# A plain second matmul in superblock 0, and zero matmuls at the start, in a one-core MLP kernel

## Chip, cores and metric

The kernel runs on one core of one Trainium2 chip. The metric is the device time of one execution in microseconds, the median of several runs.

## What is computed

Inputs are float32: x of 8 x 1024 x 1024, w1 of 1024 x 4096 and w2 of 4096 x 1024.

```python
h = x @ w1
h = 0.5 * h * (1 + np.tanh(np.sqrt(2 / np.pi) * (h + 0.044715 * h ** 3)))
return (h @ w2).astype(np.float32)
```

## The kernel before

**Superblocks and products.** The 8192 rows of x are worked off in 8 superblocks (sb) of 1024 rows. Each has two matrix products: `matmul1` gives g = gelu(x w1), kept in SBUF as four float16 blocks g11, g12, g21, g22, and `matmul2` gives the output rows. Both split their operands in 2 x 2 blocks and use a seven-product recursion: seven block products of sums and differences take the place of eight. `A_TERMS` lists the differences of the left operand, `B_TERMS` the sums of the weights; products 2 and 5 use plain weight blocks (`PLAIN`), the other five need sums (`SUMS`). One block product of a superblock is 64 matmuls of 128 x 128 by 128 x 512, so a stage is 448 matmuls. In `matmul2` from superblock 2 on, products 6 and 7 (`INNER`) are themselves split once more by `inner_product`, whose weight sums `split_inner` writes to DRAM (`in_d`) in superblock 1.

**matmul1.** It runs over 16 column chunks c of w1, four to a quad. Each chunk uses three of the eight PSUM banks (pb, qb, rb) and does 28 matmuls. ScalarE copies pb out to a tmp tile, VectorE combines tmp tiles and banks, ScalarE applies GELU. A chunk's last product (6) is done inside the next chunk (`finish`). tmp tiles come from a pool of ten, which the stores of the output also use. In superblock 0 w1 arrives as float32 in staging tiles from the pool `gc` (four buffers), is cast to float16 by ScalarE and POOL, is summed by VectorE, and its raw blocks are written to `raw_d`. Superblock 1 reads `raw_d`, makes the sums again and writes them to `w1_d` on POOL's queue. Later superblocks read `w1_d` and the plain blocks of `raw_d` (`load_ops`).

**matmul2.** Superblocks 0 and 1 use `matmul2_made`. In superblock 0 `bring` loads w2 in float32 in the order in which the products 4, 2, 5, 1, 7, 3, 6 need it, POOL casts it, `add` makes each product's sums on VectorE just ahead, and `keep` writes the raw blocks to `raw2_d`. Superblock 1 reads `raw2_d`, makes the sums a second time, writes them to `w2_d`, and splits the operands of products 7 and 6. Superblocks 2 to 7 use `matmul2` with `load_ops` from `w2_d` and `raw2_d`.

**What sets the order.** Each engine takes its instructions in a fixed order that a scheduler lays down at build time; `keep_in_program_order` (in `load_in_order`) holds SP's DMAs to the program's order, and `issue_after` puts an instruction behind another one. SP's queue carries the loads, x's transposes from DRAM (`x_transpose`) and the raw writes; POOL's queue carries the output stores, the writes of `w1_d`, `w2_d` and `in_d`, and the cast of x to float16 (`x_cast`). All share the same 16 DMA engines. An operand tile (`unit`) is one of 26 buffers of 128 x 2048 float16, 0.52 MB. At the end of superblock 0 the order on SP is: the last loads of w2, 16 transposes of x for superblock 1, eight writes of `raw2_d`, then the reads of `raw_d` for superblock 1.

**The start.** `x_first` loads superblock 0's rows in eight pieces q (four with a = 1, then four with a = 0) and transposes them on TensorE against an identity; ScalarE and VectorE copy the banks out. The first matmul follows when the first columns of w1 are cast and summed (`load_cols`).

Of the kernel before, what the change touches and what calls it, by code (L numbers as in the profile page):

```python
# [56 lines left out]
def kernel(  # L57
# [42 lines left out]
    raw2_d = [dram.tile([P, 4, QC * OH], DT, name=f"raw2_d{q}") for q in range(NI // QC)]  # L100
# [38 lines left out]
    def cast_in(dst, src, cast, staged=False):  # L139
        if staged:  # L140
            st = up.tile([P] + list(dst.shape[1:]), F32, name="u")
        else:
            st = gcp.tile([P] + list(dst.shape[1:]), F32, name="gc")
        load_in_order(st, src)
        cast(out=dst, in_=st)
# [52 lines left out]
    def load_ops(d, raw, ms, rows, cols):  # L198

        ops = {}  # L200
        for m in ms:
            t = unit(rows, cols)
            src = raw[:, BLOCKS.index(B_TERMS[m][0]), :] if m in PLAIN else d[:, m - 1, :]
            nc.sync.dma_start(out=flat(t), in_=src)
            ops[m] = t
        return ops
# [18 lines left out]

    def x_first():
        identity = consts.tile([P, P], F32, name="identity")
        make_identity(nc, identity)
        blocks = x_blocks()
        xs = XOps(blocks)  # L230
        for a in (1, 0):
            for q in range(NQ):
# [3 lines left out]
                for k in (1, 0):  # L236
                    ps = psum()
                    for j in range(KH):
                        nc.tensor.matmul(
                            ps[:, j * P:(j + 1) * P],  # L240
                            lhsT=xn[:, k, j * P:(j + 1) * P],
                            rhs=identity,
                            is_transpose=True,
                            start=(j == 0),
                            stop=(j == KH - 1),
                        )
                    eng = nc.vector.tensor_copy if k == 0 else nc.scalar.copy
                    eng(
                        out=blocks[f"{a + 1}{k + 1}"][:, :, q * P:(q + 1) * P],
                        in_=ps.rearrange("p (j t) -> p j t", t=P),  # L250
                    )
            if a:
                xs.make(2)
# [23 lines left out]
    def matmul1(xs, sb):  # L277
# [14 lines left out]
        def gelu(b, c, src):  # L292
            nc.scalar.activation(out=g[b][:, c, :], in_=src, func=GELU)  # L293
# [11 lines left out]
        def ahead(q, step):  # L305
# [3 lines left out]
            if sb > 1:  # L309
                if step == 0:  # L310
                    quads.append(load_ops(w1_d[q], raw_d[q], ORDER, KH, QW))
                return
# [6 lines left out]
            for m in ((), (4,), (1, 3), (7, 6))[step]:  # L319
                quads[q].sum(m)  # L320

# [59 lines left out]
    def matmul2_made(sb, g, keep_w1):  # L381


        raw = {b: [] for b in BLOCKS}
        sums = {}
        blocks = None

        def bring(bs, staged):
            for q in range(NI // QC):
                for b in bs:  # L390
                    t = unit(QC, OH)
                    raw[b].append(t)
                    if sb:
                        nc.sync.dma_start(out=flat(t), in_=raw2_d[q][:, BLOCKS.index(b), :])
                        continue
                    for j in range(0, QC, 2):
                        c = q * QC + j
                        cast_in(
                            t[:, j:j + 2, :],
                            w2v[int(b[1]) - 1, int(b[0]) - 1, :, c:c + 2, :],  # L400
                            pool_copy,
                            staged,
                        )
                if q == 0 and keep_w1 is not None and "11" in bs:
                    keep_w1()

        def keep(bs):
            if sb == 0:
                for b in bs:
                    for q in range(NI // QC):  # L410
                        load_in_order(raw2_d[q][:, BLOCKS.index(b), :], flat(raw[b][q]))

        def add(m):
            u, op, v = B_TERMS[m]
            sums[m] = []
            for q in range(NI // QC):
                t = unit(QC, OH)
                tt(t, raw[u][q], raw[v][q], op)
                sums[m].append(t)
                if sb:  # L420
                    nc.gpsimd.dma_start(out=w2_d[q][:, m - 1, :], in_=flat(t))

        def pieces(m):
            return raw[B_TERMS[m][0]] if m in PLAIN else sums[m]

        def copy_out(b, q, ps):
            c = temp()
            nc.scalar.copy(out=c, in_=ps)
            return store(sb, b, q, c), c

        v, c21 = {}, {}
        pb, qb, rb = [], [], []
        bring(("11", "21"), False)
        add(4)
        for q, ps in product2(g, 4, pieces(4), pb, True, True):
            v[q] = temp()
            nc.scalar.copy(out=v[q], in_=ps)
        bring(("22",), True)
        if sb == 0:
            xb = x_cast(1, pool_last[0])  # L440
        keep(("11", "21"))
        for q, ps in product2(g, 2, pieces(2), pb, False):
            _, c21[q] = copy_out("21", q, ps)
        add(1)
        u, d = halves()[1], halves()[1]
        for q, ps in product2(g, 5, pieces(5), qb, True):
            tt(u[q], v[q], ps, SUB)
            tt(d[q], u[q], c21[q], SUB)
        add(7)
        bring(("12",), True)  # L450
        for q, ps in product2(g, 1, pieces(1), rb, True):
            tt(d[q], d[q], ps, ADD)
        if sb == 0:
            blocks = x_transpose(xb, load_in_order)
        keep(("22", "12"))
        for q, ps in product2(g, 7, pieces(7), rb, False):
            c = temp()
            tt(c, u[q], ps, ADD)
            store(sb, "11", q, c)
        if sb:  # L460
            split_inner(7, pieces(7))
        add(3)
        add(6)
        for q, ps in product2(g, 3, pieces(3), qb, False):
            copy_out("12", q, ps)
        for q, ps in product2(g, 6, pieces(6), qb, False):
            c = temp()
            tt(c, d[q], ps, ADD)
            last = store(sb, "22", q, c)
        if sb:  # L470
            split_inner(6, pieces(6))
# [89 lines left out]
    def product2(g, m, pieces, banks, first, by_chunk=False):  # L561

        u, v = A_TERMS[m]

        def mm(q, a, c):
            nc.tensor.matmul(  # L566
                banks[q],
                lhsT=a,
                rhs=pieces[c // QC][:, c % QC, :],
                start=(first and c == 0),  # L570
                stop=(c == NI - 1),
                skip_group_check=not first,
            )

        if first:
            banks.extend(psum() for _ in range(NQ))
        if by_chunk:
            for c0 in range(0, NI, QC):
                for q in range(NQ):
                    for c in range(c0, c0 + QC):  # L580
                        mm(q, g[u][:, c, q * P:(q + 1) * P], c)
                    if c0 + QC == NI:
                        yield q, banks[q]
            return
        for q in range(NQ):
            cols = slice(q * P, (q + 1) * P)
            a = g[u][:, :, cols]
            if v is not None:
                a = gcp.tile([P, NI, P], GT, name="gc")
                tt(a, g[u][:, :, cols], g[v][:, :, cols], SUB)  # L590
            for c in range(NI):
                mm(q, a[:, c, :], c)
            yield q, banks[q]

    def halves():
        tiles = [up.tile([P, 2, OH], F32, name="u") for _ in range(2)]
        return tiles, [tiles[q // 2][:, q % 2, :] for q in range(NQ)]

    def matmul2(sb, g):
        def product(m, banks, first):  # L600
            pieces = [load_ops(w2_d[q], raw2_d[q], (m,), QC, OH)[m] for q in range(NI // QC)]
            return product2(g, m, pieces, banks, first)
# [7 lines left out]
        x6 = inner_x(6, g)  # L610
# [8 lines left out]
        inner_product(6, x6, d2)  # L619
        x7 = inner_x(7, g)  # L620
        for q, ps in product(3, qb, False):
            c12 = temp()
            nc.scalar.copy(out=c12, in_=ps)  # L623
            store(sb, "12", q, c12)
            tt(d[q], d[q], ps, ADD)
        for q, ps in product(1, rb, True):
            tt(u[q], u[q], ps, ADD)
            tt(d[q], d[q], ps, ADD)
            store(sb, "22", q, d[q])
        inner_product(7, x7, u2)  # L630
        for q in range(NQ):
            last = store(sb, "11", q, u[q])
        return last

    warm = consts.tile([P, 1], F32, name="warm")
# [3 lines left out]
    for sb in range(NSB):  # L639
        g, quad = matmul1(xs, sb)  # L640
        if sb and sb + 1 < NSB:
            blocks = x_transpose(x_cast(sb + 1, last), nc.sync.dma_start)
        if sb == 0:
            last, blocks = matmul2_made(sb, g, quad.keep_raw)
        elif sb == 1:
            last, _ = matmul2_made(sb, g, None)
        else:
            last = matmul2(sb, g)
# [33 lines left out]
```

## Time and profile before

| | |
|---|---|
| median of 3 runs | 1586.64 us (1584.47 to 1587.4) |
| the profiled execution's own time | 1586.64 us |
| its span, first to last instruction | 1584.9 us |
| TensorE busy | 1551.0 us, 98% |
| VectorE, ScalarE, POOL busy | 64%, 29%, 14% |
| mean granted TensorE clock | 0.994 |
| DMA | 358.93 MB, mean 226 GB/s |

PE is TensorE, PEld its weight loads, DVE VectorE, ACT ScalarE, SPq the queue of SyncE. A line of a timeline has the start, the length, the engine, the line of the code, the operation, output <- input, the count, and in brackets the idle time before it and what ended that. Stages, by the start of their first matmul: superblock 0's matmul1 at 17.52 us, its matmul2 at 122.67, superblock 1's at 220.78 and 328.18, superblock 2's at 425.59 and 529.80.

### The profile page before, as it was taken

To read this page: it belongs to the slowest core of one execution; us is meant where nothing else is said; L and a number is where in the kernel's file an instruction comes from. 1 tells how busy PE (TensorE), PEld (TensorE's weight loads), DVE (VectorE), ACT (ScalarE), POOL (GpSimd) and SP (SyncE) were. 2 spreads that over 40 slices of the span, in tenths; PEclk is the share of its full clock that TensorE was granted. 3 is DMA by queue.
4 is the path that set the end of the run, shared out by engine and by line. 5 is a ranking of instruction groups with operands and counts; after the bars stand their busy time and mean duration, and the time that the engine had idled before them with its cause. 6 is when DMAs were issued, how large, how long until landed. Compare 5 with 4: busy or idle time off the path is not lost.

```text
span 1584.9 us, 20386 instructions
## 1 busy us (share of the span) xinstructions
PE 1551.0 (98%) x7808; PEld 768.0 (48%) x7808; DVE 1010.9 (64%) x1263; ACT 457.7 (29%) x776; POOL 222.6 (14%) x306
## 2 busy tenths in 40 slices
PE   7999989999989999999999999999999999999998
PEld 4444434444434455444554445544555445544455
DVE  6877767667755566555675557656475556755564
ACT  4641014520144211441124410344103430044200
POOL 2244222012400013000120001200012001200000
PEclk9999999999999999999999999999999999999999
DMA  9998698645984467735686346954469545663155
GB/s 304 337 325 281 180 371 281 203 179 197 385 300 133 186 239 259 255 97 200 252 281 224 121 171 252 336 176 180 152 243 362 153 166 191 242 257 133 54 212 186
DMA packets 167362, 358.93 MB, mean 226 GB/s; under 512 B 72928, under 2 KB 79072, under 8 KB 166368
## 3 DMA queue, kind: packets, MB, share of 16 engines
q1 hardware_dynamic: 148672, 285.26, 51.3%
q0 software_dynamic: 18592, 72.37, 13.9%
q8 instruction: 61, 1.00, 0.2%
q14 instruction: 37, 0.30, 0.1%
HBM read 278.92 MB, written 93.32 MB: 235 GB/s over the span
## 4 chain that ended last, share of the span: by engine, by line
PE 85%; DMA 8%; DVE 4%; issue 2%; ACT 1%; POOL 0%; SPq 0%; DVEq 0%; ACTq 0%; POOLq 0%
PE ps L283 44%; PE ps L566 35%; PE ps L522 6%; DVE u L112 2%; DMA out_dram<-tmp 2%; DMA u<-w_d 2%; DMA gc<-in_w_dram 1%; DMA u<-raw_d 1%; DMA in_d<-u 1%; DVE tmp L112 1%; DMA u<-in_d 1%; DVE gc L112 0%; ACT g L293 0%; DMA u<-in_x_dram 0%; POOL in_d L487 0%
## 5 line engine op out<-in xcount | busy, mean ns | idle before, releaser
L283 PE MATMUL ps<-u 128*128 128x512 f16 x3584 | 784.2, 381 | 20.5 <-DVE tmp L112 15.3
L112 DVE TENSOR_TENSOR tmp<-tmp,ps 128x512 f32<-128x512 f32 x548 | 375.5, 687 | 307.4 <-ACT tmp L347 119.9
L283 PEld LDWEIGHTS <-u 128*128 128x128 f16 x3584 | 351.7, 98 | 450.8 <-issue 29.5
L566 PE MATMUL ps<-u,gc 128*128 128x512 f16 x1792 | 389.4, 379 | 0.0
L566 PEld LDWEIGHTS <-gc 128*128 128x128 f16 x1792 | 175.3, 98 | 211.5
L293 ACT ACTIVATE g<-tmp 128x512 f16<-128x512 f32 x256 | 161.0, 630 | 296.7 <-DVE tmp L112 296.7
L566 PE MATMUL ps<-u,g 128*128 128x512 f16 x1024 | 224.4, 379 | 0.4 <-DVE u L112 0.2
L293 ACT ACTIVATE g<-ps 128x512 f16<-128x512 f32 x256 | 151.9, 596 | 102.3 <-PE ps L283 102.1
L112 DVE TENSOR_TENSOR u<-u 128x2048 f16<-128x2048 f16 (+2 forms) x150 | 162.9, 1122 | 20.5 <-DMA u<-raw_d 12.5
L566 PEld LDWEIGHTS <-g 128*128 128x128 f16 x1024 | 100.2, 98 | 120.7 <-issue 1.9
L112 DVE TENSOR_TENSOR gc<-g,g 128x2048 f16<-128x2048 f16 x112 | 136.7, 1253 | 20.5 <-PE ps L566 20.5
L379 POOL DMA_DIRECT2D out_dram<-tmp x72 | 39.6, 551 | 778.3 <-ACT tmp L616 632.3
L112 DVE TENSOR_TENSOR u<-u,ps 128x512 f32<-128x512 f32 x152 | 101.2, 682 | 71.1 <-ACT tmp L623 37.3
L522 PE MATMUL ps<-u,gc 128*128 128x256 f16 x960 | 110.6, 274 | 0.8
L522 PEld LDWEIGHTS <-gc 128*128 128x128 f16 x960 | 94.4, 98 | 13.3 <-issue 1.9
L347 ACT COPY tmp<-ps 128x512 f32<-128x512 f32 x128 | 73.0, 570 | 93.6 <-PE ps L283 93.6
L112 DVE TENSOR_TENSOR gc<-u 128x2048 f16<-128x2048 f16 x60 | 73.2, 1221 | 38.9 <-PE ps L566 38.9
L112 DVE TENSOR_TENSOR tmp<-ps,tmp 128x512 f32<-128x512 f32 x128 | 88.4, 690 | 9.7 <-DMA out_dram<-tmp 4.0
L112 DVE TENSOR_TENSOR u<-tmp,ps 128x512 f32<-128x512 f32 x32 | 22.0, 687 | 83.6 <-PE ps L566 73.9
L112 DVE TENSOR_TENSOR u<-g,g 128x2048 f16<-128x2048 f16 x48 | 59.6, 1280 | 0.0
L616 ACT COPY tmp<-ps 128x512 f32<-128x512 f32 x24 | 14.1, 587 | 151.9 <-PE ps L566 151.9
L545 POOL TENSOR_TENSOR u<-u,tmp 128x512 f32<-128x512 f32 x12 | 26.2, 2180 | 200.1 <-DMA u<-in_d 141.4
(33 smaller groups left out, 354.1 us busy)
## 6 DMA issues: line engine op xcount, KB each, us to landing
u<-w_d SPq DMA_DIRECT2D x192, 512.0 KB, 8.3
u<-raw_d SPq DMA_DIRECT2D x128, 512.0 KB, 8.1
u<-in_d SPq DMA_DIRECT2D x84, 512.0 KB, 7.2
gc<-in_w_dram SPq DMA_DIRECT2D x48, 512.0 KB, 6.2
w_d<-u POOLq DMA_DIRECT2D x40, 512.0 KB, 6.9
out_dram<-tmp POOLq DMA_DIRECT2D x72, 256.0 KB, 3.1
raw_d<-u SPq DMA_DIRECT2D x32, 512.0 KB, 7.5
xb<-in_x_dram POOLq DMA_DIRECT2D x56, 256.0 KB, 11.4
```

Of the source, the lines that this page charges most:

```text
L112: nc.vector.tensor_tensor(out=out, in0=in0, in1=in1, op=op)
L283: nc.tensor.matmul(bank, lhsT=ops[m][:, k, cs], rhs=xs[m][:, k, :], start=(first and k == 0), stop=(k == KH - 1), skip_group_check=not first,)
L293: nc.scalar.activation(out=g[b][:, c, :], in_=src, func=GELU)
L347: nc.scalar.copy(out=v, in_=pb)
L379: return queue.dma_start(out=out2[r0:r0 + P, o0:o0 + OH], in_=src)
L522: nc.tensor.matmul(bank[:, i * HO:(i + 1) * HO], lhsT=t[:, c, i * P:(i + 1) * P], rhs=y[j][:, c, :], start=(first and i == 0 and c == 0), ...
L545: nc.gpsimd.tensor_tensor(out=part("11"), in0=part("11"), in1=pair(u), op=ADD)
L566: nc.tensor.matmul(banks[q], lhsT=a, rhs=pieces[c // QC][:, c % QC, :], start=(first and c == 0), stop=(c == NI - 1), skip_group_check=not ...
L616: nc.scalar.copy(out=c21, in_=ps)
```

## The change

- Superblock 0's second matmul (`matmul2_first` in place of `matmul2_made`) is a plain product: two halves b of the output columns, each with eight PSUM banks (all there are), 16 chunks c of w2 rows and both row halves a: 512 matmuls. The last three chunks (`TAIL`) are done bank by bank, and ScalarE copies each bank out as it ends. w2 arrives half by half in the `gc` staging buffers. POOL casts the first two quads of half 0; ScalarE casts all else, and only after the last GELU (`act_late_copy`).
- In half 1 VectorE makes all five sums of each quad, and SP writes all seven operands to `w2_d`: quads 0 and 1 between the loads, quads 2 and 3 behind x's transposes. `raw2_d` is gone.
- Superblock 1's second matmul is now `matmul2`, which reads `w2_d`. It does its products in the order 4, 5, 2, 3, 1, 6, 7 without the inner recursion, and splits the operands of 6 and 7 for later superblocks. x for superblock 2 is transposed as for the later ones.
- `matmul1` of superblock 1 also writes the two plain operands of each quad to `w1_d` (`copy_plain`, 8 writes more); later superblocks read all seven from there.
- `keep_clock` issues matmuls on a zero tile into one PSUM bank: 8 before the first transposes, 2 after each piece of x, 6 after the last piece.

```diff
+    def act_late_copy(out, in_):
+        with tc.issue_after(gelu_last[0].ins):
+            nc.scalar.copy(out=out, in_=in_)
...
+        def copy_plain(self):
+            for m in PLAIN:
+                nc.gpsimd.dma_start(out=w1_d[self.q][:, m - 1, :], in_=flat(self.ops[m]))
...
+    def keep_clock(bank, n):
+        for _ in range(n):
+            tc.keep_in_program_order(
+                nc.tensor.matmul(bank, lhsT=idle[:, :P], rhs=idle, start=True, stop=True)
+            )
...
+        idle_bank = psum()
+        keep_clock(idle_bank, 8)
...
+                keep_clock(idle_bank, 2 if a or q < NQ - 1 else 6)
...
+            if sb == 1 and step == 3:
+                quads[q].copy_plain()
...
+    def matmul2_first(sb, g, keep_w1):
+        TAIL = 3
...
+        def write(q):
+            for m in SUMS + PLAIN:
+                load_in_order(w2_d[q][:, m - 1, :], flat(made[q][m]))
+
+        for b in range(2):
+            banks = [psum() for _ in range(2 * NQ)]
+            ready = []
...
+            for q in range(NI // QC):
+                raw = raw_units(QC, OH, (b + 1,))
+                for j in range(0, QC, 2):
+                    c = q * QC + j
+                    for a in range(2):
+                        cast_in(
+                            raw[f"{a + 1}{b + 1}"][:, j:j + 2, :],
+                            w2v[b, a, :, c:c + 2, :],
+                            pool_copy if b == 0 and q < 2 else act_late_copy,
+                        )
+                for j in range(QC):
+                    w = [raw[f"{a + 1}{b + 1}"][:, j, :] for a in range(2)]
+                    ready.append(w)
+                    if q * QC + j < NI - TAIL:
+                        for i in range(2 * NQ):
+                            mm(i, q * QC + j, w)
+                if b == 0:
+                    keep.append(raw)
+                    if q == 0:
+                        keep_w1()
+                    elif q == 1:
+                        xb = x_cast(1, pool_last[0])
+                else:
+                    ops = {}
+                    for m in SUMS + PLAIN:
+                        make_sum(ops, m, {**keep[q], **raw}, QC, OH)
+                    made.append(ops)
+                    if q in (1, 2):
+                        write(q - 1)
+            if b == 1:
+                blocks = x_transpose(xb, load_in_order)
+                write(2)
+                write(3)
+            for i in range(2 * NQ):
+                for c in range(NI - TAIL, NI):
+                    mm(i, c, ready[c])
+                o = temp()
+                nc.scalar.copy(out=o, in_=banks[i])
+                last = store(sb, f"{i // NQ + 1}{b + 1}", i % NQ, o)
         return last, blocks
...
         if sb == 0:
-            last, blocks = matmul2_made(sb, g, quad.keep_raw)
-        elif sb == 1:
-            last, _ = matmul2_made(sb, g, None)
+            last, blocks = matmul2_first(sb, g, quad.keep_raw)
         else:
+            if sb + 1 < NSB:
+                blocks = x_transpose(x_cast(sb + 1, last), nc.sync.dma_start)
             last = matmul2(sb, g)
```

## The prediction

> **What bounds the kernel now.** I read the totals first, then busy time by stage, then TensorE's timeline where a stage is long, and last the chain of waits and SP's queue there. The totals:
>
> ```profile
> span 1584.9 us, 20386 instructions
> PE 1551.0 (98%) x7808; PEld 768.0 (48%) x7808; DVE 1010.9 (64%) x1263; ACT 457.7 (29%) x776; POOL 222.6 (14%) x306
> ```
>
> TensorE is busy for 98%, so the end moves by matmuls added or removed and by TensorE's few stops. Busy time by stage shows where those are; the first two columns are the stretch and its length, the last three the granted clock, the DMA share and GB/s.
>
> ```profile
> 17.52:122.67 105.15, 101.35 (x448) 44.36 (x449) 84.34 (x113) 58.25 (x94) 39.77 (x36) 0.97 0.94 323
> 122.67:220.78 98.11, 97.13 (x449) 43.73 (x448) 67.72 (x63) 8.27 (x14) 30.16 (x36) 1.00 0.82 252
> 220.78:328.18 107.40, 99.88 (x448) 44.19 (x449) 78.17 (x104) 44.83 (x78) 17.82 (x34) 0.97 0.74 251
> 328.18:425.59 97.41, 97.18 (x450) 43.80 (x448) 73.31 (x83) 8.27 (x14) 27.20 (x48) 1.00 0.68 258
> 425.59:529.80 104.21, 98.23 (x449) 44.19 (x448) 54.99 (x80) 45.49 (x78) 6.11 (x12) 0.98 0.66 220
> 623.62:720.31 96.69, 96.69 (x450) 43.84 (x448) 55.00 (x80) 45.69 (x78) 5.62 (x12) 1.00 0.62 202
> ```
>
> Each row is one matmul stage of 448 instructions. The last is undisturbed: 96.69 / 448 = 0.2158 us per matmul. Against it the first matmul of superblock 0 loses 8.5 us, superblock 0's second 1.4, superblock 1's first 10.7, its second 0.7, superblock 2's first 7.5. TensorE's timeline shows the two large losses as stops after a stage boundary:
>
> ```profile
> 206.01 13.98 PE L566 MATMUL ps<-u,gc 128*128 128x512 f16 x64
> 220.78 3.63 PE L283 MATMUL ps<-u 128*128 128x512 f16 x16 [0.79 <-DVE u L112]
> 229.08 9.15 PE L283 MATMUL ps<-u 128*128 128x512 f16 x32 [4.67 <-DVE tmp L112]
> ...
> 425.59 10.52 PE L283 MATMUL ps<-u 128*128 128x512 f16 x48
> 442.09 87.87 PE L283 MATMUL ps<-u 128*128 128x512 f16 x400 [5.98 <-DVE tmp L112]
> ```
>
> VectorE is named, but the chain of waits says why it is late (start, length, what), and SP's timeline says why the reads were:
>
> ```profile
> 210.65 10.20 DMA u<-raw_d
> 228.05 12.91 DMA out_dram<-tmp
> 427.55 13.68 DMA out_dram<-tmp
> ...
> 178.12 21.48 SPq L120 DMA_TRANSPOSE u<-xb  x16
> 199.64 8.31 SPq L120 DMA_DIRECT2D raw_d<-u  x8
> ```
>
> SP issues x's 16 transposes, then eight writes of raw w2, and only at 208.05 the reads of raw w1 that superblock 1's first sums need; stores then take 12.9 and 13.7 us in a full DMA system (shares 1.04 and 1.05 in 220.78:245.99 and 425.59:442.09), and each holds a tmp buffer that VectorE's next output needs.
>
> **The plain second matmul.** It removes 448 matmuls of the recursion and adds 16 chunks x 16 banks x 2 = 512: 64 x 0.2158 = +13.8, all on the path. The removed stage lost 1.4 us. I allow the new one 0.8 for its two handovers of all eight banks, so it is 512 x 0.2158 + 0.8 = 111.3 instead of 98.1: **+13.2**. ScalarE takes 24 of the 32 casts of w2 from POOL; they wait for the last GELU and then cost 24 x 1.04 = 25 us of an engine that is busy for 8.27 of 98.11 us. Behind them wait its bank copies and, through the staging buffers, SP's next loads. The 20 sums of w2 on VectorE stay as many, and its differences of g and output sums in this stage go: nothing. Halfway, half b = 1 needs banks that ScalarE copies, and in the built order three of its in-order casts of w2 stand between the copies of banks 3 and 7. With T the stage's start, bank 7 ends at T + 55. A buffer of the four-deep gc pool turns round in 6.2 (median landing of gc<-in_w_dram) + 1.04 (ScalarE's cast) = 7.3 us, so the groups of four loads are cast at about T + 6, 13, 20 and 27. The write of quad 0's seven operands stands in SP's queue ahead of the next group, and its first slots must land (7.5, raw_d<-u), so that group is cast at T + 37 and the last lands at T + 50. That is 5 us of slack; the stage may lose 0.4 to 7.
>
> **SP's queue at the first boundary.** Transposes stand behind those loads, so they start at about T + 44 and take 21.5 us as now, to T + 66. Writes of quads 2 and 3 (14 x 0.52 MB, at 400 GB/s 1.3 us each, 18 us) follow, to T + 84, and the reads of raw w1 for quad 0 land at about T + 90, for quad 1 at T + 97. Five sums each at 1.27 are done by T + 104; the stage ends at T + 111. At present those reads land 1 us before the boundary. VectorE's first tmp output waits in order behind quad 1's sums and behind the first two reads of quad 2 (landing about T + 106), needed at T + 113. POOL's queue also helps: the eight last stores wait behind seven writes of w1_d that wait for quad 0's sums, and these are early. I keep 0.7 us here, and 1.3 for the later wait on quad 3's reads (now one such stop of 1.12 us at 264.62). So 107.4 becomes 98.7: **-8.7**; bounds 97.0 (-10.4) and 107.4 (0).
>
> **The second boundary.** Superblock 1 now reads finished operands of w2 instead of making them: 20 sums and 20 writes of 0.52 MB leave its second matmul (10 us of DMA time in the last 27 us for the eight of m = 3 and 6). 16 reads become 28, spread over the stage. The splits for the inner recursion stand in VectorE's order before the last product's outputs, so their writes leave before the last stores on POOL, and quad 0 of w1 is requested a product (13.8 us) before the boundary. What is late next is the last store, c11 of q = 3, issued at the boundary itself; its buffer is needed 9 us later, and a 6.5 us landing (median of out_dram<-u) covers that. I take 0.8 us lost of the 7.5: **-6.7**; bounds 0.2 (-7.3) and 7.5 (0). Superblock 1's second matmul keeps 0.3 of its 0.7: **-0.4**. Eight more w1_d writes (two plain operands in four quads) add 10.5 us of DMA time to a 97 us stage at share 0.74: nothing, with the 1.3 above as what it may add.
>
> **The start.** Busy time in short stretches:
>
> ```profile
> 4.00:6.00 2.00, 1.55 (x8) 1.58 (x9) 0.00 (x0) 0.42 (x1) 0.00 (x0) 1.00 0.98 385
> 8.00:10.00 2.00, 1.86 (x17) 1.62 (x15) 1.48 (x3) 1.12 (x2) 0.00 (x0) 1.00 1.02 420
> ...
> 20.00:24.00 4.00, 4.00 (x11) 1.45 (x10) 4.00 (x6) 0.93 (x2) 1.65 (x2) 0.50 1.09 345
> 26.00:28.00 2.00, 2.00 (x11) 0.93 (x10) 0.93 (x2) 1.56 (x3) 1.80 (x2) 1.00 0.23 51
> ```
>
> The granted clock is 0.50 at 20 to 24, where 11 matmuls take 0.36 to 0.43 each; the twelve between 19.68 and 25.0 cost 2.6 us more than at full clock. The GELU behind them delays ScalarE's casts, the casts hold the gc buffers, and at 26 to 28 DMA falls to a share of 0.23: 1.5 us of transfer lost in a stretch bound by w1's arrival. The zero tile: 8 matmuls before x (8 x 0.43 = 3.4 us from 1.1, over when x lands at 4.45: nothing), 2 between transposes (0.43 us, against 0.21 to 0.27 us of waiting per q from 10.14 on: +0.2 each, 0.6 us later at 15.1), 6 at the end (1.3 us, covered by the wait for the first operands, at most 0.6 past 17.52). If the clock holds, the dip goes: -1.3, by the 1.5 lost less what stays; bounds -2.6 and +0.6. Two stops of 0.17 and some VectorE sums before 122.67 go with the recursion, -0.4. Together **-1.7**.
>
> The Trainium skill ("TensorE: Matmul & The Clock Gate", Part 4) says transposes do not count as a busy TensorE. The rows differ: 8 transposes in 1.55 us at 4 to 6 and 17 in 1.86 at 8 to 10, so they did speed up. By the page any zero matmuls help and the start gives its -1.3; by the row the idle stretch from 15.1 to 17.5 did it, which the last six shorten to about 1.1 us, also -1.3. Part 1 of the same page makes an idle window of about 3.4 us the condition, which would leave this gap harmless and the start worth +0.6; the 0.50 in the row speaks against it.
>
> **Sum.** +13.2 - 8.7 - 6.7 - 0.4 - 1.7 = -4.3, from a span of 1584.9 to 1580.6. The profiled execution took 1586.64, 1.7 more than its span, and is the median run, so I predict 1582.3. All best bounds: 12.8 - 10.4 - 7.3 - 0.7 - 3.0 = -8.6, 1578.0.
>
> **Rivals.**
> - The first boundary's stop stays. If every transfer of the plain stage is 10 us later (28 writes against the recursion's 16, and that stage's DMA share is 0.82 already), quad 1's reads land after T + 107 and VectorE's queue stands behind them; from about 8 us of lateness on it decides. Price 8.7: 1591.0, slower. For it: SP's order is one queue. Against: the first 40 us of DMA work is bound by four buffers, not bandwidth. 18%.
> - The second boundary's stop stays, as w1's reads and the split's writes still meet there (share 1.02 at 410:430): +6.7, 1589.0. 10%.
> - The handover in the middle of the plain stage waits for the last casts: from 5 us of lateness on, price up to 6: 1588.3. 6%.
> - The zero tile does not hold the clock, or only lengthens the transposes: +1.9, 1584.2. 6%.
>
> The forecast, with nearly all stops gone, has 60%, and its own range is 1578 to 1586.5.
>
> **How the numbers follow.** The range goes from the best bounds to the first rival with 2 us more, leaving out its pairs with the others: 1578 to 1593. About 0.2% (3.2 us) is what a measurement here can tell from no change: 1583.5 and 1589.8 are the bounds. Of the forecast's 60% two thirds lie below 1583.5, its middle being 1.2 under that, and 3 of the clock rival's and the handover's: 0.43. The first rival and the pairs of the second and third give 0.24 slower; 0.33 remain.
>
> **What would show it.** Right: 512 matmuls in about 111.3 us for superblock 0's second matmul, raw w1 reads landing 10 us or more before it ends, no stop over 1 us on tmp in the next stage, a superblock 2 first matmul under 99 us, a granted clock of 1.00 from 18 to 26 and no DMA dip at 26. Wrong: a stop of TensorE on a ScalarE copy in the plain stage's middle, or on tmp outputs behind raw w1 reads at either boundary.

## The result: slower by 0.6%

| | before | changed kernel |
|---|---|---|
| median of 4 runs each, one chip | 1587.02 us | 1596.28 us |
| lowest and highest | 1584.47, 1587.75 | 1595.50, 1598.14 |
| profiled execution (span) | 1586.64 (1584.9) | 1595.98 (1594.2) |

The ratio is 1.0063, 95% interval 1.0045 to 1.0080, so the change costs about 10 us where I had forecast a gain of 4.3. The time lies outside my range. (Times of the later experiments are ratios to the kernel before on the same chip.)

The totals of the changed kernel's profile answer the two of before:

```profile
span 1594.2 us, 20535 instructions
PE 1567.3 (98%) x7900; PEld 775.8 (49%) x7900; DVE 948.7 (60%) x1204; ACT 485.0 (30%) x804; POOL 184.1 (12%) x270
```

TensorE has 92 matmuls more, 64 of the plain stage and 28 on the zero tile, and is busy for 16.3 us more; its share is the same. Busy time by stage (columns as before: stretch, length, PE, PEld, DVE, ACT, POOL, granted clock, DMA share, GB/s) shows where the time went:

```profile
18.33:121.82 103.49, 99.93 (x448) 44.08 (x449) 82.08 (x111) 58.37 (x94) 30.66 (x34) 0.98 0.95 310
121.82:234.68 112.86, 110.89 (x514) 50.10 (x513) 39.12 (x36) 34.13 (x41) 9.73 (x18) 1.00 0.95 318
234.68:344.56 109.88, 101.21 (x450) 44.78 (x449) 66.44 (x92) 45.98 (x79) 17.88 (x34) 0.95 0.75 259
344.56:441.25 96.69, 96.69 (x449) 43.84 (x448) 53.40 (x66) 8.29 (x14) 19.57 (x33) 1.00 0.68 251
441.25:537.94 96.69, 96.69 (x449) 43.83 (x448) 55.10 (x80) 45.69 (x78) 4.48 (x9) 1.00 0.61 199
```

Four of the five rows are within 2 us of the prediction. The third, superblock 1's first matmul, is not: it was to fall from 107.4 to 98.7 us and rose to 109.9. Of the 13.2 us that it loses against 96.69, TensorE's timeline shows 8.67 as two stops; the other 4.5 are matmuls at a granted clock that averages 0.95 in the row (busy 101.21 instead of 96.69; behind the stops it is 0.50 from 244.42 to 248 and 0.60 from 279.76 to 284).

```profile
121.82 57.58 PE L416 MATMUL ps<-u,g 128*128 128x512 f16 x266
180.53 0.59 PE L416 MATMUL ps<-u,g 128*128 128x512 f16 x2 [1.13 <-ACT tmp L461]
181.96 52.88 PE L416 MATMUL ps<-u,g 128*128 128x512 f16 x244 [0.84 <-ACT tmp L461]
234.68 4.48 PE L298 MATMUL ps<-u 128*128 128x512 f16 x20
244.42 31.93 PE L298 MATMUL ps<-u 128*128 128x512 f16 x136 [5.26 <-DVE tmp L111]
279.76 64.96 PE L298 MATMUL ps<-u 128*128 128x512 f16 x292 [3.41 <-DVE tmp L111]
```

The chain of waits names the transfers behind the last two lines: reads of raw w1.

```profile
166.19 12.66 DMA gc<-in_w_dram
...
235.90 6.55 DMA u<-raw_d
...
266.02 11.17 DMA u<-raw_d
```

SP's timeline has their origin. The first landing of raw w1 for quad 0 lets VectorE start at 222.53, which is T + 100.7 on the prediction's scale (T = 121.82), quad 1's last sums start at 233.51 (T + 111.7), and the read that completes quad 2's first pair lands at 242.45 (T + 120.6). Predicted were 90, 97 and 106, with 113 as the moment when the third is needed.

```profile
155.03 7.72 SPq L119 DMA_DIRECT2D w_d<-u  x7
164.91 4.11 SPq L119 DMA_DIRECT2D gc<-in_w_dram  x4
170.20 27.29 SPq L119 DMA_TRANSPOSE u<-xb  x16
197.53 15.94 SPq L119 DMA_DIRECT2D w_d<-u  x14
213.52 55.21 SPq L163 DMA_DIRECT2D u<-raw_d  x16
```

Which of the things that end together at 242 to 244 had to go? I had four theories before the experiments. Q: SP's order (raw w1 behind 14 writes of w2). V: VectorE's order (sums of w1 for quads 1 and 2 stand ahead of the first tmp outputs). S: POOL's order (the eight last stores stand behind quad 0's writes of w1, and hold tmp buffers). B: the bytes, since the DMA system is full there whatever the order.

### The profile page after: what moved, and what is told of

Same layout as the page of the kernel before. It is cut to its first block, busy times and chain, and to the rows that moved or that the text cites. A ratio compares the mean times of both kernels' runs of the same rounds, so it can differ in the third digit from the quotient of the medians.

```text
span 1594.2 us, 20535 instructions
## 1 busy us (share of the span) xinstructions
PE 1567.3 (98%) x7900; PEld 775.8 (49%) x7900; DVE 948.7 (60%) x1204; ACT 485.0 (30%) x804; POOL 184.1 (12%) x270
## 4 chain that ended last, share of the span: by engine, by line
PE 88%; DMA 7%; DVE 2%; ACT 1%; issue 1%; SPq 1%; POOL 0%; DVEq 0%; ACTq 0%
PE ps L298 46%; PE ps L566 32%; PE ps L513 6%; PE ps L416 3%; DMA gc<-in_w_dram 3%; DMA u<-w_d 2%; DVE u L111 1%; DMA u<-raw_d 1%; DMA w_d<-u 1%; ACT u L141 1%; SPq L119 0%; DMA u<-in_d 0%; DVE tmp L111 0%; DVE gc L111 0%; DMA u<-in_x_dram 0%
## 5 line engine op out<-in xcount | busy, mean ns | idle before, releaser
L566 PE MATMUL ps<-u,gc 128*128 128x512 f16 x1472 | 320.0, 379 | 0.0
L566 PEld LDWEIGHTS <-gc 128*128 128x128 f16 x1472 | 144.1, 98 | 173.6
L566 PE MATMUL ps<-u,g 128*128 128x512 f16 x896 | 195.7, 379 | 0.0
L111 DVE TENSOR_TENSOR u<-u 128x2048 f16<-128x2048 f16 (+2 forms) x130 | 136.4, 1087 | 85.9 <-ACT u L141 42.2
L308 ACT ACTIVATE g<-ps 128x512 f16<-128x512 f32 x256 | 152.3, 597 | 97.0 <-PE ps L298 96.7
L566 PEld LDWEIGHTS <-g 128*128 128x128 f16 x896 | 87.6, 98 | 104.5
L111 DVE TENSOR_TENSOR gc<-g,g 128x2048 f16<-128x2048 f16 x92 | 109.4, 1222 | 6.5 <-PE ps L566 6.5
L416 PE MATMUL ps<-u,g 128*128 128x512 f16 x512 | 111.0, 379 | 2.0 <-ACT tmp L461 2.0
L513 PEld LDWEIGHTS <-gc 128*128 128x128 f16 x960 | 93.7, 98 | 13.6 <-issue 1.6
L416 PEld LDWEIGHTS <-g 128*128 128x128 f16 x512 | 50.1, 98 | 62.8 <-issue 2.7
```

The lines of the kernel that those rows point to most:

```text
L111: nc.vector.tensor_tensor(out=out, in0=in0, in1=in1, op=op)
L308: gelu_last[0] = nc.scalar.activation(out=g[b][:, c, :], in_=src, func=GELU)
L416: nc.tensor.matmul(banks[i], lhsT=g[f"{i // NQ + 1}{a + 1}"][:, c, (i % NQ) * P:(i % NQ + 1) * P], rhs=w[a], start=(c == 0 and a == 0), st ...
L513: nc.tensor.matmul(bank[:, i * HO:(i + 1) * HO], lhsT=t[:, c, i * P:(i + 1) * P], rhs=y[j][:, c, :], start=(first and i == 0 and c == 0), ...
L566: nc.tensor.matmul(banks[q], lhsT=a[:, c, :], rhs=pieces[c // QC][:, c % QC, :], start=(first and c == 0), stop=(c == NI - 1), skip_group_ ...
```

## Experiments

A common measure: the **three stages** from the start of superblock 0's second matmul to the start of superblock 2's first, in the profiled execution. The second boundary's gain, in superblock 2's first matmul, lies behind them. Before: 302.9 us (122.67 to 425.59); changed kernel: 319.4 (121.82 to 441.25); the prediction: 307.0; with no stop at all, 303.9 with the plain stage (512 x 0.2158 + 2 x 96.69) and 290.1 with the recursion (3 x 96.69).

| kernel | ratio to before, 95% | three stages |
|---|---|---|
| changed kernel | 1.0063 (1.0045 to 1.0080) | 319.4 |
| 1 sums late | 1.0024 (1.0014 to 1.0033) | 313.9 |
| 2 no late writes of w2 | 0.9976 (0.9967 to 0.9985) | 306.3 |
| 3 recursion, finished operands | 0.9968 (0.9955 to 0.9981) | 306.3 |
| 4 the same, sums late | 0.9973 (0.9963 to 0.9983) | 309.7 |
| 5 sums late, stores by ScalarE | 1.0018 (1.0009 to 1.0028) | 316.2 |
| 6 reads of raw w1 first | 1.0068 (1.0054 to 1.0082) | 322.2 |
| 7 the three of 1, 5, 6 | 1.0025 (1.0012 to 1.0038) | 318.2 |
| 8 zero tile on before | 1.0007 (0.9998 to 1.0016) | (start alone) |
| 9 sums late, w1's writes deferred | 0.9992 (0.9982 to 1.0002) | 311.0 |
| 10 recursion, writes deferred | 0.9995 (0.9985 to 1.0005) | 314.4 |
| 11 recursion, both | 0.9927 (0.9913 to 0.9941) | 299.3 |
| 12 writes deferred alone | 1.0030 (1.0016 to 1.0043) | 320.3 |

One profiled execution need not be the median of its kernel (runs of one kernel here spread by 3 to 9 us), so the ratios decide and the stages say where.

**1. Sums late.** In superblock 1 the sums of w1 are issued after the chunk's last output (`out_last` is its c11 sum, set for superblock 1 alone):

```diff
+        with ExitStack() as late:
+            if out_last[0] is not None:
+                late.enter_context(tc.issue_after(out_last[0].ins))
             tt(ops[m][:, :, sl], raw[u][:, :, sl], raw[v][:, :, sl], op)
```

> The changed kernel, but in superblock 1 VectorE's sums of w1 for quads 1 to 3 are issued after the last output (c11) of the chunk that asks for them; every transfer keeps its place. Theory V (the reads of raw w1 are late, but they stop TensorE only because VectorE's queue has the sums of quads 1 and 2 ahead of the first tmp outputs): the stops of 5.26 us at 244 and 3.41 us at 280 go, and with them the half-clock stretches behind them; superblock 1's first matmul is 98 to 100 us instead of 109.9, the time about 1585. Theory B (the DMA system is full from 200 to 262 us, whatever VectorE does): operands of quad 1 or tmp buffers held by slow stores stop TensorE instead; the stage stays over 104, the time at 1590 or more.

Median 1591.12 us, and the stage took 105.2 (233.79 to 339.00), as theory B had it. The second stop is gone, as theory V had it, and the first became longer. The chain of waits shows what stood right behind VectorE's sums:

```profile
230.09 0.52 POOL w_d L208
230.61 13.79 DMA out_dram<-tmp
...
244.53 0.70 DVE tmp L111
...
245.27 14.91 PE ps L303 x62
```

The first of the last eight stores was issued only after POOL had issued seven writes of w1_d, which wait for the late raw reads; then it took 13.79 us to land, and VectorE's next tmp buffer came with it. TensorE's stop is 7.00 us, ending within 1 us of the changed kernel's (245.27 and 244.42).

**2. No late writes.** `write(2)` and `write(3)` are taken out.

```diff
                 blocks = x_transpose(xb, load_in_order)
-                write(2)
-                write(3)
...
-            pieces = [load_ops(d, (m,), QC, OH)[m] for d in w2_d]
+            pieces = [load_ops(d, (m,), QC, OH)[m] for d in w2_d[:2] * 2]
```

> The changed kernel without the 14 writes of w2's operands for quads 2 and 3 (later superblocks read quads 0 and 1 twice in their place, so this part of the output is another one). SP's queue then has nothing between x's transposes and the reads of raw w1, and 7.3 MB of writes are gone. Theory Q (SP's queue makes raw w1 late): the reads start about 16 us earlier, at 197 instead of 213.5, VectorE has quad 1's and quad 2's first operands before 234, and superblock 1's first matmul is 97 to 99 us; the time about 1584. If VectorE's order alone mattered and the reads were late for another reason (the loads of w2 or the transposes), 104 or more stay.

Median 1583.00 us; superblock 1's first matmul took 97.4 us (232.48 to 329.90), with one stop of 0.37. With VectorE's and POOL's orders as in the changed kernel, leaving out 14 writes takes both stops away. That is Q or B: order and bytes were taken out together.

**3 and 4. The recursion kept.** Superblock 0 keeps the kernel before's recursion, with the sums of w2 written out as they are made and plain blocks 11 and 22 kept; superblock 1 reads them and does its splits as in the changed kernel. Kernel 4 has the sums late as well.

```diff
-                if sb:
-                    nc.gpsimd.dma_start(out=w2_d[q][:, m - 1, :], in_=flat(t))
+                nc.gpsimd.dma_start(out=w2_d[q][:, m - 1, :], in_=flat(t))
...
-        keep(("11", "21"))
+        keep(("11",))
...
-        keep(("22", "12"))
+        keep(("22",))
...
-        elif sb == 1:
-            last, _ = matmul2_made(sb, g, None)
         else:
             last = matmul2(sb, g)
```

> The kernel before with only the second boundary's part of the change: superblock 0's second matmul stays the recursion, but writes finished operands of w2 (20 sums on POOL's queue, 8 plain blocks on SP's), and superblock 1 reads them as in the changed kernel. If the parts are independent: superblock 0's second matmul 98 to 99 us, superblock 1's second 96.7 and superblock 2's first 97 (instead of 97.4 and 104.2); superblock 1's first stays at 107.4 plus or minus 4, since 12 writes more cross that boundary. The time about 1579, 1575 to 1583. If the second boundary's gain came from the plain stage or from the eight copies of w1's plain operands, superblock 2's first matmul stays over 102.

> The recursion kernel of the run before with superblock 1's sums of w1 issued after the chunk's last output. Theory V: both boundaries' stops go, superblock 1's first matmul is 98 to 100 us, the time about 1570 (1568 to 1574). Theory B: the stage stays over 104, the time at 1575 or more.

Medians 1582.97 and 1582.69 us. In kernel 3 superblock 1's second matmul and superblock 2's first take 96.7 us each: the second boundary's gain needs neither the plain stage nor the copies of w1's plain operands. The first boundary is worse than before (the three stages take 306.3 us instead of 302.9); 12 more writes cross it, which would explain that, but no run shows it by itself. Its two largest stops in TensorE's timeline:

```profile
223.28 5.31 PE L283 MATMUL ps<-u 128*128 128x512 f16 x16 [4.06 <-DVE u L112]
231.40 8.75 PE L283 MATMUL ps<-u 128*128 128x512 f16 x32 [2.81 <-DVE tmp L112]
```

Kernel 4 missed its 1570 by 13 us: as in kernel 1, behind VectorE's sums stood a store (issued 231.93, 13.13 us to land).

**5. Stores by ScalarE.** Kernel 1, with seven of the eight last stores on ScalarE's queue.

```diff
         queue = nc.gpsimd if sb < NSB - 1 else nc.sync
+        if sb == 0 and b[1] == "2" and (b, q) != ("22", 3):
+            queue = nc.scalar
```

> The kernel with superblock 1's sums of w1 issued late (first experiment), and besides, the first seven of the eight last stores of the plain stage are issued by ScalarE, which has just copied their banks, instead of by POOL, where they stand behind seven writes of w1's operands. In the first experiment the first of these stores was issued at 230.6 and landed at 244.4, and a tmp buffer for VectorE came with it. Theory S (the stores on POOL's queue wait for raw w1 and hold the tmp buffers): they leave at 226 to 234 and land by 240, the stop of 7.0 us falls under 1.5, superblock 1's first matmul is 97.5 to 100 us instead of 105.2, the time about 1584. Theory B (the DMA system is full, the queue does not matter): the stores take longer in proportion and 4 us or more of stop stay; 1588 or more.

Median 1590.12 us: theory S fell, at least as the whole. The stop moved to 247, and behind it is a store that waited for nothing but its bank's copy:

```profile
235.03 0.59 ACT tmp L469
235.63 0.02 issue
235.65 15.48 DMA out_dram<-tmp
...
251.25 0.70 DVE tmp L111
```

A 256 KB store takes 15.48 us there, against a median of 3.7 for all 72 of these stores in the changed kernel. The queue from which a transfer is issued did not help. The Trainium skill says so ("DMA: Bandwidth & Descriptors", "Issuing engines are not separate DMA queues"): DMAs of all issuing engines run on the same 16 DMA engines and interleave, so that another issuer saves sequencer time alone. This run agrees.

**6 and 7. Reads first.** SP's order alone is changed (`MadeQuad` issues the reads of a quad's raw w1); kernel 7 adds the edits of 1 and 5.

```diff
                 blocks = x_transpose(xb, load_in_order)
+                early.append(MadeQuad(0, False))
                 write(2)
+                early.append(MadeQuad(1, False))
                 write(3)
```

> The changed kernel with another order on SP's queue alone: after x's transposes come the reads of raw w1 for quad 0, then the writes of quad 2 of w2, the reads for quad 1, the writes of quad 3; the same transfers and bytes. Theory Q (order): quad 0's reads land at about 206 and quad 1's at about 220 instead of 222 to 234, POOL's writes for quad 0 and with them the last stores are no longer held up, superblock 1's first matmul is 97.5 to 99.5 us, the time about 1585. Theory B (bytes): with 7.3 MB of writes still in the same stretch the stores or the reads of quad 2 are late instead and the stage keeps 104 or more; 1590 or more.

> The three together: reads of raw w1 for quads 0 and 1 ahead on SP, superblock 1's sums late on VectorE, seven of the last stores on ScalarE's queue. Theories Q, V and S each leave nothing to stop the stage: 96.7 to 98 us, the time about 1583.5. Theory B: 102 or more, the time over 1588.

Medians 1597.99 and 1591.42 us: theory Q fell, in both. Quad 0's reads did land earlier (POOL issues its first write of w1 at 204.29 instead of 222.94), but VectorE could not use them. VectorE's timeline of kernel 6:

```profile
216.78 5.89 DVE L111 TENSOR_TENSOR u<-u 128x2048 f16<-128x2048 f16 x5 [30.83 <-DMA w_d<-u]
225.99 3.50 DVE L111 TENSOR_TENSOR u<-u 128x2048 f16<-128x2048 f16 x3 [3.31 <-DMA w_d<-u]
230.52 8.04 DVE L111 TENSOR_TENSOR u<-u 128x2048 f16<-128x2048 f16 x7 [1.03 <-DMA w_d<-u]
248.00 1.23 DVE L111 TENSOR_TENSOR u<-u 128x2048 f16<-128x2048 f16 x1 [9.45 <-DMA u<-raw_d]
```

The sums wait for writes of w2 to land, since the writes hold the u buffers that the sums need; TensorE stops for 13.71 us. Reads that go ahead take the place of writes in the same full system, and 26 buffers tie the one to the other. In kernel 7, with the sums late and the stores on ScalarE's queue, a stop of 5.42 us stays behind a store that takes 15.40 to land, and in the chain of waits this store stands behind a write that took 16.23. What the buffers alone cost was not separated: more of them were not tried.

**8. The zero tile alone**, in the kernel before.

> The kernel before with nothing but the zero tile's matmuls at the start. If they hold the clock as predicted: 1.3 us earlier at superblock 0's second matmul, a granted clock of 1.00 from 18 to 26, the time about 1586. If, as the changed kernel's trace suggests (0.62 and 0.53 at 20 to 24), they only move the half clock by one stretch: within 0.8 us of before at that point, the time the same within 0.1%.

Median 1588.42 us, the same as before. Superblock 0's second matmul starts 0.45 us earlier (122.22); kernels 3 and 4, without a zero tile, start it at 121.90 and 122.13, so even that need not be the zero tile's doing. The half clock still comes, after the last six zero matmuls:

```profile
18.00:20.00 2.00, 1.01 (x5) 0.29 (x6) 1.49 (x2) 0.64 (x2) 1.91 (x2) 0.94 1.15 298
20.00:22.00 2.00, 2.00 (x5) 0.70 (x6) 2.00 (x4) 0.98 (x2) 0.27 (x1) 0.50 0.96 277
22.00:24.00 2.00, 2.00 (x8) 0.75 (x6) 2.00 (x3) 0.00 (x0) 2.00 (x2) 0.71 1.07 368
```

The mean granted clock from 18 to 26 is 0.79 here and in the changed kernel, and 0.57 in the kernel before; but kernels 3, 4 and 11, without a zero tile, also have 0.79 (kernel 10: 0.64). In the other traces with the zero tile the clock often holds: it is 1.00 through this whole stretch in kernels 1, 5, 6, 7 and 9 (kernel 2: 0.97, kernel 12: 0.79). Five of nine traces with the zero tile, and none of five without, make an effect on the clock likely, though each kernel has one trace. It gains no time that can be seen. Kernel 1 and the changed kernel differ in superblock 1 alone; here are their rows, kernel 1 first:

```profile
19.90 2.76 PE L303 MATMUL ps<-u 128*128 128x512 f16 x12 [1.01 <-POOL u L122]
24.80 3.41 PE L303 MATMUL ps<-u 128*128 128x512 f16 x15 [2.13 <-DVE u L111]
```

```profile
20.35 4.45 PE L298 MATMUL ps<-u 128*128 128x512 f16 x12 [0.98 <-POOL u L122]
25.25 7.70 PE L298 MATMUL ps<-u 128*128 128x512 f16 x34 [0.45 <-DVE u L111]
```

In kernel 1, at the full clock, the twelve matmuls take 1.7 us less, and TensorE then waits 1.7 us longer for VectorE's sums: in both kernels the next matmul comes 4.90 us after the first of the twelve. Superblock 0's second matmul starts at 121.76 in kernel 1 and at 121.82 in the changed kernel.

**9 and 12. w1's writes deferred.** The seven writes of a quad's operands are issued by ScalarE behind the GELUs of the quad's second and third chunk, instead of by POOL as soon as they are made; in 9 with the sums late, in 12 alone. `g11` is the chunk's last GELU.

```diff
-            if not self.first:
-                nc.gpsimd.dma_start(out=w1_d[self.q][:, m - 1, :], in_=flat(self.ops[m]))
+        def write_out(self, part):
+            for m in (SUMS + PLAIN)[part]:
+                nc.scalar.dma_start(out=w1_d[self.q][:, m - 1, :], in_=flat(self.ops[m]))
...
+            if sb == 1 and j in (1, 2):
+                with tc.issue_after(g11.ins):
+                    quads[q].write_out(slice(0, 3) if j == 1 else slice(3, None))
```

> The kernel with superblock 1's sums late on VectorE (first experiment), and the seven writes of w1's operands of each quad deferred: ScalarE issues them behind the GELUs of the quad's second and third chunk, instead of POOL as soon as they are made, ahead of the last stores. Theory B (the transfers between the transposes' end at 197.5 and the first outputs do not fit: 14 writes of w2, 10 reads of raw w1, 7 writes of w1 and 8 stores are 18.4 MB, 45 us at 410 GB/s, to 242): 3.7 MB of these go behind, 9 us; the stores leave as soon as they are copied, the stop of 7.0 us falls under 1, superblock 1's first matmul is 97.5 to 100 us, the time about 1584. If the stretch is short of something else (SP's issue, the 26 buffers of the u pool), 4 us or more of stop stay and the time is 1588 or more.

Median 1585.33 us, where B said 1584: 11 us under the changed kernel. TensorE has no stop in superblock 1's first matmul until the next stage's first reads. The DMA view of 198 to 245 (busy tenths in 40 slices, then the sum) shows the difference, first the changed kernel, then this one:

```profile
DMA  7999999999999999899999999999999999999999
...
DMA packets 5342, 18.28 MB, mean 389 GB/s; under 512 B 903, under 2 KB 903, under 8 KB 5340
```

```profile
DMA  9999999999999998999999999865978989997989
...
DMA packets 4105, 15.65 MB, mean 333 GB/s; under 512 B 575, under 2 KB 575, under 8 KB 4007
```

The changed kernel keeps the DMA system full for all 47 us; with 2.6 MB less there it has slack from about 228 on. A full system does not stop TensorE by itself, though. Kernel 2 is almost as full in the same 47 us, and TensorE loses 0.37 us there:

```profile
DMA packets 4867, 17.94 MB, mean 382 GB/s; under 512 B 618, under 2 KB 618, under 8 KB 4823
```

Its first read of raw w1 was issued at 196.31 instead of 213.52, and what fills the rest is mostly POOL's traffic (11.70 MB). So theory B holds for the bytes that go ahead of a needed transfer, not for all bytes of the stretch; that the expectation's sum of 18.4 MB came near the 18.28 of the trace says little, as a full stretch of 47 us moves about that much whatever it carries. The edit also takes these writes out of the stores' way on POOL's queue; experiment 5 had shown that a free way for seven of the stores does not end the stop.

> The changed kernel with the deferred writes of w1's operands alone; VectorE's sums of w1 stay where they were, those of quad 1 and one of quad 2 ahead of the first outputs. With the changed kernel, the sums late (first experiment) and both together (ninth) this closes the square. If the bytes in the stretch are the whole cause, it is as fast as both together: superblock 1's two stages within 1.5 us of 197.7, the time about 1585.5. If VectorE's order stops TensorE by itself, since the operands of quads 1 and 2 wait for buffers and reads whatever the stores do: a stop of 3 us or more on tmp stays, the two stages take 201 to 206, the time 1589 to 1595.

Median 1593.88 us, the second case. The square of the changed kernel is closed: by the ratios, times 1587, it is +10.0 us with neither, +3.8 with the sums late, +4.8 with the writes deferred, -1.3 with both, so that by the medians each takes away its part and the parts add up (3.8 + 4.8 - 10.0 = -1.4, known to about 4 us by the intervals). In the profiled executions superblock 1's two stages take 206.6, 201.9, 205.1 and 197.7 us in the same order, where deferring alone gains only 1.5; kernel 12's was the slowest of its seven runs. Both views agree that VectorE's order costs time with and without the deferral, and that the whole gain needs both edits. In kernel 12 VectorE's chain has a new link, a buffer that a deferred write holds:

```profile
252.24 7.01 DMA w_d<-u
...
259.33 1.20 DVE u L111
```

**10 and 11. The recursion with deferred writes**, in 11 with the sums late: the edit of 9 on kernels 3 and 4, with five writes of a quad.

> The recursion kernel (third experiment: superblock 0 keeps the recursion and writes finished operands of w2) with the five writes of w1's operands of each quad deferred in the same way. Theory B: superblock 1's first matmul, 112.5 us there, loses 2.6 MB of 410 GB/s traffic, 6 us, ahead of its first outputs and its stores no longer stand behind those writes: 100 to 106 us, the time about 1574 (1570 to 1578). If something else holds it, 110 or more, the time about 1582.

> As the run before, and superblock 1's sums late on VectorE (fourth experiment). Theory B with VectorE's order: 98 to 103 us for superblock 1's first matmul, the time about 1572. If VectorE's order is no part of it: the same as the run before within 2 us.

Medians 1586.95 and 1574.70 us. Kernel 10 missed by 13 us: deferring alone made kernel 3 slower, by 0.27%, with a stop of 4.68 us on the same kind of link as in kernel 12 (a w1 write issued at 242.45, 8.55 us, then a sum, then tmp). Kernel 11 met its expectation within 3 us. Here the two edits do not add up: by the ratios it is -5.1 us with neither, -4.3 with the sums late, -0.8 with the writes deferred, -11.6 with both. Either edit alone leaves a wait that stands in the chain (a store in kernel 4, a deferred write in kernel 10). Kernel 11 is the fastest, 0.73% under before and 1.35% under the changed kernel. Its first boundary still has two stops, one of them on raw w1:

```profile
221.32 5.13 PE L290 MATMUL ps<-u 128*128 128x512 f16 x16 [4.24 <-DVE u L112]
228.30 92.95 PE L290 MATMUL ps<-u 128*128 128x512 f16 x428 [1.84 <-DVE tmp L112]
```

## Why the prediction was wrong

| term of the sum | predicted | measured |
|---|---|---|
| plain second matmul | +13.2 | +14.75 |
| first boundary (superblock 1's first matmul) | -8.7 | +2.48 |
| second boundary (superblock 2's first matmul) | -6.7 | -7.52 |
| superblock 1's second matmul | -0.4 | -0.72 |
| start and superblock 0's first matmul | -1.7 | -0.85 |
| the rest, to the end of the span | 0 | +1.2 |
| sum | -4.3 | +9.3 |

- **The step that failed is "SP's queue at the first boundary"**, 11.2 of the 13.6 us. I named the right chain, in the right order, and the point at which it decides (8 us of lateness), and then timed it too short by 14.6 us. The pieces of these 14.6, for quad 2's first pair of reads: the transposes ended at T + 75.7 instead of T + 66 (9.7: they started 4.4 later and took 27.3 instead of 21.5 us); the 14 writes took 16 instead of 18 (-2); and from there to that landing it was 29 instead of 22 (+7). Two things are missing from my reckoning of the last piece. I let SP's transfers have the 400 GB/s to themselves, while POOL issued eight writes of w1 and six stores, 5.8 MB, into the same DMA system before 242.45. And I took it that a read leaves as soon as SP reaches it: SP had issued the eight reads of quads 0 and 1 by 220.5, but quad 2's two only at 228.56 and 235.90, after waits for an earlier read's landing and for VectorE's sums (6.9 us before the second), which free u buffers. The second then landed within 6.55 us, the shortest of these reads. How the 7 us divide between shared bandwidth and buffers, no run shows.
- **"POOL's queue also helps" was the opposite.** The sentence held only if quad 0's sums were early. They were late, and the seven writes ahead of the stores became a second line of waits that ends at the same time as VectorE's (experiment 1). Deferring these writes helps (9); whether by their bytes, their place on POOL's queue or their buffers was not separated.
- **The rival had it, at 18%.** I called it "every transfer of the plain stage is 10 us later" and argued against it that the first 40 us are bound by four buffers, not bandwidth. Bound by buffers or not, they were late, and the transposes started 4.4 us late behind them; why these then took 5.8 us longer, at a DMA share of 0.73 from 182 to 198, stays open (in kernels 3 and 4 they took 24.5 and 28.4). The bandwidth is short later, from 198 to 245. Its price, 8.7, was too low as well: it was the forecast gain given up, and the stage came out 11.2 us over the forecast, with longer stops (8.67) and the half clock behind each (4.5).
- **The plain stage** came out 1.6 us longer: its handover lost 1.97 us on ScalarE's bank copies, not 0.8 with both handovers, since the last load of w2 landed at T + 57 and not T + 50 (12.66 us in the chain). This is the third rival in a milder form, at the lateness that I gave for it. The prediction had one wait for a write's landing ahead of the last loads (7.5 us) and gave the issuing of the writes no time; SP took 7.56 and 7.72 us for the two sets of seven.
- **The second boundary was right in mechanism and nearly in size**: 96.69 us and no stop. Experiment 3 shows that finished operands alone do it.
- **The start was wrong in its mechanism, though small.** I had put the half clock on the path: 2.6 us of matmul time, 1.5 us of lost transfer. Kernel 1 shows that the path there is VectorE's sums: with a granted clock of 1.00 the next matmul waits 2.13 us for them and comes 4.90 us after the first of the twelve. In the kernel before the twelve took 5.32 us, so some 0.4 of the 2.6 us was on the path. The dip in DMA stays too (a share of 0.56 at 24 to 26 in kernel 1). The clock itself is not settled by the gap, as I had it: with gaps of 1.16 and about 1.0 us it fell in the changed kernel (0.62 and 0.53 at 20 to 24) and held in kernel 1. The zero tile alone gave no time (8).
- **The end** was not in the sum. After the last output SP waits 2.7 us for TensorE's sequencer, 0.7 before; 2.0 of the 9.3 us lie there, less 0.8 that the rest of the run gains. In the experiments this wait was 0.7 to 2.8 us with no pattern that I can name, and it stays open.

## What to carry to other kernels

Where a queue's order decides, time it by all that is in flight: add up the bytes that every queue puts between the last slack and the transfer that is needed, and divide by the rate that the trace shows when full (here 18.4 MB by experiment 9's list, at 389 GB/s 47 us, where SP's 24 transfers alone are 31 at the prediction's 400 GB/s), and ask for each transfer whether its buffer is free when its turn comes. When that sum did not fit here, moving one thing gave at most a part: VectorE's order 6 of the 10 us, w1's writes about 5 by the medians, the issuer of the stores or the place of the reads nothing. What took the stops away were 14 writes fewer (2), or later writes together with VectorE's sums late (9); one line of in-order waits that is opened shows the next one behind it. Before paying 14 us of matmuls for a better boundary, try the boundary's part of the edit alone: experiment 3 had the second boundary's whole gain without them, at the price of about 3 us more in the three stages ahead of it.

## What I had not expected of the hardware

- The 256 KB stores that stood in the chains of kernels 1, 4, 5 and 7 took 13.1 to 15.5 us to land in the full stretch, whichever engine issued them, against a median of 3.7 over the changed kernel.
- The full DMA system moved 389 GB/s on average over 47 us (18.28 MB), and single slices reach 436. The Trainium skill ("DMA: Bandwidth & Descriptors", "Bandwidth") gives about 358 GB/s as the bound for transfers between HBM and SBUF, as a core's share when both cores of an HBM domain stream, and 425 GB/s for a 16 MB load by one core alone. One core runs here: the 389 lies between the two, and the slices come up to the 435 that the page gives for the ports.
- In the changed kernel the half clock came at 20 us with gaps of only 1.16 and 0.98 us in TensorE's work. In kernel 1, with gaps of 1.16 and 1.01 at the same place, the granted clock was 1.00 from 18 to 26. So these gaps do not decide it, and what does stays open.
- A half clock need not cost time: in the changed kernel the twelve matmuls took 4.45 us instead of kernel 1's 2.76, and the next one still had to wait for VectorE (0.45 us).
